# A four-layer decoder trunk in f32 on one core: other opening pieces, chunk 3 loaded into idle tiles, the bias table written from SyncE's queue, lambda later, no low parts on POOL

## The chip, the cores and the metric

The kernel runs on one core of one Trainium2 chip. The metric is the device time of a run in microseconds, from the first to the last instruction of the program on that core; lower is better. Engines are named as the profile names them: PE is TensorE, DVE is VectorE, ACT is ScalarE, POOL is GpSimd, SP is SyncE, which here only issues DMAs. A "queue" is the row of DMAs that one engine issues, in order.

## The reference, cut to what matters

Input x is 256 tokens by 1024. Four residual layers follow each other, the first being the even mixer; only that layer's beginning is touched by what follows.

```
h = x
for layer in range(4):                       # DEPTH 2 in the code: mixer + FFN, twice
    h = h + (even_mixer or odd_mixer)(rmsnorm(h, norm1), w_in, ..., w_out)
    h = h + conv_ffn(rmsnorm(h, ffn_norm), w_in, conv_w, conv_b, w_out)
return rmsnorm(h, final_norm)

even_mixer(h):                               # q,k,v of 8 heads (width 64) and of 4 differential heads
    qa, ka, va, qd, kd, vd = split_cols(h @ w_in, ...)
    o_a = softmax(qa ka' * scale + bias[head] , causal) va
    lam = exp(sum(lp0*lp1)) - exp(sum(lp2*lp3)) + lam_init
    o_b = rmsnorm((softmax(q0 k0') - lam * softmax(q1 k1')) vd) * (1 - lam_init)
    return concat(o_a, o_b) @ w_out
```

The bias of a head is a row of a small table, looked up by the distance of query and key.

## The kernel before, in words

**Weights in chunks.** `PLAN` lists all weights as chunks of 128 x 2048 f32 (1 MB) in the order in which PE wants them: chunk 0 is `eq0` (queries of the first heads), 1 `ek0`, 2 `eq1`, 3 `ek1`, 4 and 5 `eva0`, `eva1` (values), 6 on `eq2` and so forth. `load_raw` brings a chunk from HBM into one of three `raw` buffers by SP's queue. `split_piece` then makes two tiles of each piece: ACT rounds it to `whi` (line 147), and DVE subtracts that from the raw piece to get `wlo` (line 148). For 7 pieces (the second of chunks 6, 9, 12, 15, 51, 57 and 60) the subtraction is POOL's. Activations are split alike, into `xh` and `xl` (tile `xs`). Each product is three passes on PE: whi·xh, whi·xl, wlo·xh. All matmuls of the weights go through the helper at line 123, so they are told apart by the tile that they write: `pd` (queries, keys, FFN), `pv` (values), `pS` (scores), `pT` (transposed probabilities), `acc` (output projection).

**The opening.** PE starts with warm-up matmuls (`warm`). x (tile `hT`) and chunks 0 and 1 come in parts along the contraction, as `FIRST_KS` cuts them: parts of 1, 1, 2, 2, 2 of the eight blocks of 128 rows, so pieces of 128, 128, 256, 256, 256 KB. Of each part `passmajor` runs first whi·xh on both halves of chunk 0 and then on both of chunk 1, then whi·xl in the same order, then wlo·xh. One block gives 4 x 3 = 12 matmuls of 128x256, so a part of two blocks 24. What follows on PE is fixed by hand: `psbt` (bias rows), eq1 (48 matmuls), `pss` (column sums for the norm), the first half of ek1, `psb` (spreads the norm over partitions, from the DVE tile `diag`), the second half of ek1, `pS` of heads 0 to 3, the values of eva0 and eva1 (24 matmuls of 128x512), `pS` of heads 4 to 7, 24 more, then `pT`, eq2 and so on.

**DMA order.** Every DMA from SP or ACT signals on one of eight semaphores in turn; one that takes a semaphore still in use waits for the DMA of eight before to land. In the listings these waits are DMAHW0 to DMAHW7. An engine that waits for a semaphore holds everything behind it in its own order, DMA issues among them.

**The bias table and lambda.** DVE adds the mask to the rows (`ar_t`), ACT's queue writes them to DRAM (`btab`), and ACT's queue reads them back shifted by partition into `Tt` (`bias_load`, heads 0 to 7 in one DMA of 1 MB). DVE's `sc` adds `Tt` to the scores; `ex` are the probabilities, `rd` the inverse of their sum. `lambdas` computes lam on DVE and ACT from `lam_t`, 128 KB on SP's queue; it stands right behind `u3`'s other work.

Of the kernel before, what the change touches and what calls it, by code (L numbers as in the profile page):

```python
# [21 lines left out]
F32 = mybir.dt.float32  # L22
F32R = mybir.dt.float32r
AF = mybir.ActivationFunctionType
ALU = mybir.AluOpType
# [11 lines left out]
NBIAS = 20  # L37
NTAB = 384
# [5 lines left out]
RAW_AHEAD = 3  # L44
LAG = 2
LAGF = 4
WARM = 10
FIRST = 4
FIRST_KS = ((0, 1), (1, 2), (2, 4), (4, 6), (6, 8))
POOLSHARE = 3  # L50
NARROW = 5
TAIL = ((0, 0, 512), (0, 512, 1024), (1, 0, 512), (1, 512, 768), (1, 768, 1024))

# [3 lines left out]
NSMALL = 36  # L57
NCONV = 4 * NF
# [40 lines left out]
PLAN = _plan()  # L99
# [3 lines left out]
def trunk(ctx, tc, x, rel_bias, small, lam_p, wpack, fin_g, onehot, addrow, tab, out):  # L103
    nc = tc.nc
    consts = ctx.enter_context(tc.tile_pool(name="consts", bufs=1))
# [13 lines left out]
    def t2(name, dt=F32, shape=(128, 2, S)):  # L119
        return two.tile(list(shape), dt, name=name, tag="t2")  # L120
# [8 lines left out]
    chunks, raws, splits = {}, {}, {}  # L129
    index = {p[0]: i for i, p in enumerate(PLAN)}  # L130

    def pieces(i):
        n = PLAN[i][4] * PLAN[i][6]
        if i < 2:
            return n, [slice(a * S, b * S) for a, b in FIRST_KS]
        return n, [slice(c, c + 1024) for c in range(0, n, 1024)]

    def load_raw(i, part=None, eng=None):
        n, ps = pieces(i)
        if i not in raws:  # L140
            raws[i] = wraw.tile([128, 2048], F32, name="raw")
        s = slice(0, n) if part is None else ps[part]
        (eng or nc.sync).dma_start(raws[i][:, s], wpack[i, :, s])

    def split_piece(i, s, eng=None):
        hi, lo, raw = splits[i], splits[i, 1], raws[i]
        nc.scalar.activation(hi[:, s], raw[:, s], AF.Copy)  # L147
        (eng or nc.vector).tensor_tensor(lo[:, s], raw[:, s], hi[:, s].bitcast(F32), op=ALU.subtract)  # L148

    def open_split(i):  # L150
        name, nk, ncol = PLAN[i][0], PLAN[i][4], PLAN[i][6]
# [5 lines left out]

    def split_chunk(i):
        open_split(i)
        for n, s in enumerate(pieces(i)[1]):  # L160
            pool = PLAN[i][0][0] in "eo" and n == 1 and i % POOLSHARE == 0 and i > 4
            split_piece(i, s, nc.gpsimd if pool else None)

    raw_at, split_at = [2], [2]

# [28 lines left out]
    def load_x(part, eng):  # L194
        k = slice(*FIRST_KS[part])
        eng.dma_start(hT[:, k], x[:, k])
    load_x(0, nc.sync)
    load_raw(0, 0)
    load_raw(1, 0, nc.scalar)
    load_x(1, nc.sync)  # L200
    load_raw(0, 1, nc.scalar)
    load_raw(1, 1)
    load_x(2, nc.scalar)
    for part in range(2, len(FIRST_KS)):
        if part > 2:
            load_x(part, nc.sync)
        for i in range(2):
            load_raw(i, part)
        if part == 3:
            rb = consts.tile([32, NBIAS], F32)  # L210
            nc.sync.dma_start(rb, rel_bias)
            oh_t = t2("oh_t", shape=(32, NTAB))
            nc.sync.dma_start(oh_t, onehot)
            ar_t = t2("ar_t", shape=(NBIAS + 1, NTAB))
            nc.sync.dma_start(ar_t, addrow)
    load_raw(2, 0)
    load_raw(2, 1)

    lam = consts.tile([128, 4], F32)
    subg = consts.tile([128, 1], F32)  # L220
# [101 lines left out]
    def bias_load(h0, n, at):  # L322
        nc.scalar.dma_start(Tt[:, at:at + n], bass.AP(tensor=btab.tensor, offset=btab.offset + h0 * NTAB,
                                                      ap=[[1, 128], [NTAB, n], [1, S]]))
        return {h0 + i: Tt[:, at + i] for i in range(n)}
# [202 lines left out]
    def v_units(env, cname, vname):  # L528
        ts = []

        def run(tb):
            need(cname + '0')
            c = [chunks[cname + '0'], need(cname + '1')]
            p = bank("pv")
            vjob(p, tb, c)
            t = t2(vname, shape=(128, 512))
            nc.scalar.activation(t, p, AF.Copy, scale=env['r_col'][:, tb:tb + 1])
            ts.append(t)
            if tb == 1:
                env[vname] = ts  # L540
        return [(None, lambda: run(0)), (None, lambda: run(1))]
# [20 lines left out]
    def proj_units(prefix, order, store):  # L562
        box = {}

        def unit(i):
            kt = order[i]

            def run():
                if i == 0:
                    box['acc'] = [bank("acc") for _ in range(4)]  # L570
                proj_tile(box['acc'], store[kt], need(f"{prefix}{kt // 2}"), kt % 2, i == 0, i == KD - 1)
            return kt, run
        return [unit(i) for i in range(KD)], box

    def lambdas():
        for i in range(2):
            nc.vector.tensor_tensor(lam_t[:, 0:64] if i == 0 else lam_t[:, 128:192],
                                    lam_t[:, 128 * i:128 * i + 64],
                                    lam_t[:, 128 * i + 64:128 * i + 128], op=ALU.mult)
            nc.vector.reduce_sum(lam[:, 1 + i:2 + i], lam_t[:, 128 * i:128 * i + 64],  # L580
                                 axis=mybir.AxisListType.X)
        nc.scalar.activation(lam[:, 1:3], lam[:, 1:3], AF.Exp)
        nc.vector.tensor_sub(lam[:, 3:4], lam[:, 1:2], lam[:, 2:3])
        nc.vector.tensor_scalar(lam[:, 0:1], lam[:, 3:4], LAM_INIT, None, op0=ALU.add)

    def even_layer():
        env, store = {}, {}
        T = T0
        box = {}

        def u1():
            c = chunks['eq1']
            p = box['q1'] = bank("pd")
            colmajor([(p[:, 0:S], True, c, 0)])
            split_chunk(3)
            split_at[0] = 4

        def u2():
            p = box['q1']
            colmajor([(p[:, S:], True, chunks['eq1'], 128)])  # L600
            stats1(env)

        def u3():
            box['k1'] = bank("pd")
            colmajor([(box['k1'][:, 0:S], True, chunks['ek1'], 0)])
            p = box['q1']
            stats2(env)
            stats_q(env)
            evac_pair(env, first[0], ('q0', 'q1'), env['r_q'])
            evac_pair(env, first[1], ('k0', 'k1'), env['r_bc'])  # L610
            evac_pair(env, p, ('q2', 'q3'), env['r_q'])
            split_chunk(4)
            split_at[0] = 5
            begin.close()
            lambdas()
            nc.gpsimd.tensor_tensor(sel, iot, iot, op=ALU.mult)
            nc.gpsimd.tensor_scalar(sel, sel, 4096.0, None, op0=ALU.is_equal)
            nc.gpsimd.tensor_tensor(sel, sel, ident, op=ALU.add)
            T.update(bias_load(8, 4, 8))

        def u4():
            colmajor([(box['k1'][:, S:], True, need('ek1'), 128)])
            evac_pair(env, box['k1'], ('k2', 'k3'), env['r_bc'])

        units = [(None, u1), (None, u2), (None, u3), (None, u4)]
        units += v_units(env, 'eva', 'va')
        units += qk_units(env, 'eq2', ('q4', 'q5'), 'r_q') + qk_units(env, 'ek2', ('k4', 'k5'), 'r_bc')
        units += qk_units(env, 'eq3', ('q6', 'q7'), 'r_q') + qk_units(env, 'ek3', ('k6', 'k7'), 'r_bc')
        units += v_units(env, 'evd', 'vd')
        pu, pbox = proj_units('e_o', list(range(8)), store)  # L630
        units += pu
        tasks = [pair_task(env, f"q{i}", f"k{i}", T, 2 * i, 'va', i * 128, store, i)
                 for i in range(4)]
        tasks += [diff_task(env, f"q{4 + i}", f"k{4 + i}", T, 8 + i, 'vd', i * 128, store, 4 + i)
                  for i in range(4)]
        interleave(env, units, tasks, store, FIRST)
        close_phase(pbox['acc'], NORM2[0])
# [336 lines left out]
            split_piece(i, pieces(i)[1][part])  # L974
        passmajor(items, range(a, b))
    pb = bias_rows()
    open_split(2)
    split_piece(2, pieces(2)[1][0])
    bias_add(pb)
    split_piece(2, pieces(2)[1][1])  # L980
    nc.scalar.dma_start(btab, ar_t)
    for j in range(4):
        square_tile(j, hT[:, 2 * j:2 * j + 2], nc.vector)
    for i in (3, 4, 5):
        load_raw(i)
    raw_at[0] = 6
    split_at[0] = 3
    lam_t = t2("lam_t", shape=(128, 256))
    nc.sync.dma_start(lam_t, bass.AP(tensor=lam_p.tensor, offset=lam_p.offset,
                                       ap=[[0, 128], [1, 256]]))  # L990
    ccol = [consts.tile([128, NCONV], F32, name=f"ccol{l}") for l in range(2)]
    for l in range(2):
        nc.sync.dma_start(ccol[l], small[:, NSMALL + l * NCONV:NSMALL + (l + 1) * NCONV])
    tab_t = consts.tile([128, S], F32)
    nc.sync.dma_start(tab_t, tab)
    T0 = bias_load(0, 8, 0)
    even_layer()
    ffn(0, False)
    odd_layer()
# [71 lines left out]
```

## Time and profile before

| | us |
|---|---|
| median of 3 runs (599.11 to 600.66) | 599.34 |
| profiled execution, its own time | 603.9 |
| its span, first to last instruction | 602.1 |
| PE busy (98% of the span) | 589.1 |
| DVE, ACT, POOL busy | 438.7, 349.4, 88.6 |

The profiled execution is one run with the profiler on; its span is what the rows below are cut from, and its time holds 1.8 us around the span. Busy times overlap each other, so they don't add up to the span.

### The profile page before, as it was taken

How to read it: one execution, taken by the hardware profiler on the slowest of the kernel's cores; microseconds unless marked ns; L12 is line 12 of the kernel's file. 1: busy time of each engine (PE TensorE's matmuls, PEld its weight loads, DVE VectorE, ACT ScalarE, POOL GpSimd, SP SyncE). 2: the span in 40 equal slices, each digit the busy share in tenths (PEclk: the TensorE clock that was granted, in tenths of full speed). 3: DMA queues.
4: the chain of work that ended last, by engine and by line, in shares of the span. 5: the costliest groups of instructions: out<-in, count | busy, mean ns of one | idle time of the engine just before them, and what ended most of it. 6: DMA issues, size and time to landing. Idle time of an engine off the chain costs nothing.

```text
span 602.1 us, 10377 instructions
## 1 busy us (share of the span) xinstructions
PE 589.1 (98%) x4078; PEld 542.3 (90%) x4078; DVE 438.7 (73%) x784; ACT 349.4 (58%) x645; POOL 88.6 (15%) x88
## 2 busy tenths in 40 slices
PE   8989999999999999999999999999999999999996
PEld 8878999999999999999999998999988888888885
DVE  5598657689877787777787884658967787777752
ACT  6549557466655565555664574736655566655632
POOL 1010122032111010011142111004111111011110
PEclk9999999999999999999999999999999999999999
DMA  7976644435455545544545333344545545554301
GB/s 235 330 256 222 238 177 157 142 127 189 175 211 210 183 174 203 201 161 169 180 167 205 145 140 140 141 140 158 219 149 209 210 162 188 211 181 170 139 1 71
DMA packets 20250, 106.67 MB, mean 177 GB/s; under 512 B 2463, under 2 KB 6249, under 8 KB 8425
## 3 DMA queue, kind: packets, MB, share of 16 engines
q1 hardware_dynamic: 16396, 101.63, 46.8%
q10 hardware_dynamic: 3644, 3.85, 2.0%
q8 instruction: 32, 0.52, 0.4%
q0 software_dynamic: 160, 0.52, 0.3%
q14 instruction: 18, 0.14, 0.1%
HBM read 104.92 MB, written 1.08 MB: 176 GB/s over the span
## 4 chain that ended last, share of the span: by engine, by line
PE 88%; DVE 5%; DMA 3%; issue 2%; ACT 1%; POOL 1%; POOLq 0%; SPq 0%; ACTq 0%; DVEq 0%
PE pd L123 51%; PE acc L123 26%; PE pv L123 4%; DVE wlo L148 2%; PE pO L123 2%; PE pS L123 2%; DMA lam_t<-in_lam_dram 1%; DMA hT<-in_x_dram 1%; PE puq L123 1%; DVE ex L358 1%; PE pukv L123 0%; DVE sc L348 0%; PE psb L123 0%; PE pT L362 0%; PE pss L123 0%
## 5 line engine op out<-in xcount | busy, mean ns | idle before, releaser
L123 PE MATMUL pd<-xs,whi 128*128 128x256 f32 (+1 forms) x1312 | 329.2, 330 | 1.6 <-ACT whi L147 1.4
L123 PE MATMUL pd<-xs,wlo 128*128 128x256 f32 x928 | 256.6, 281 | 0.0
L148 DVE TENSOR_TENSOR wlo<-raw,whi 128x1024 fp32r<-128x1024 f32 (+2 forms) x190 | 232.2, 1248 | 24.0 <-ACT whi L147 23.9
L123 PEld LDWEIGHTS pd<-xs,whi 128*128 128x128 f32 x1312 | 219.8, 190 | 24.6 <-ACT whi L147 2.6
L147 ACT ACTIVATE whi<-raw 128x1024 fp32r<-128x1024 f32 (+2 forms) x197 | 196.4, 1023 | 58.1 <-PE pd L123 18.2
L123 PEld LDWEIGHTS pd<-xs,wlo 128*128 128x128 f32 x928 | 174.3, 190 | 0.1
L123 PE MATMUL acc<-o,whi 128*128 128x256 f32 x608 | 108.7, 281 | 0.0
L123 PEld LDWEIGHTS acc<-o,whi 128*128 128x128 f32 x608 | 92.7, 188 | 1.0 <-issue 0.2
L123 PE MATMUL acc<-o,wlo 128*128 128x256 f32 x304 | 84.7, 279 | 0.0
L786 POOL TENSOR_TENSOR ge<-ge,gbuf 128x256 f32<-128x256 f32 x44 | 37.1, 844 | 291.2 <-ACT ge L785 291.2
L890 ACT ACTIVATE lowp<-pd 128x256 f32<-128x256 f32 x68 | 25.9, 381 | 79.8 <-PE pd L123 79.8
L891 DVE TENSOR_TENSOR ug<-pd,lowp 128x256 f32<-128x256 f32 x68 | 28.5, 419 | 50.4 <-ACT lowp L890 50.4
L123 PE MATMUL acc<-whi,o 128*128 128x512 f32 (+1 forms) x220 | 58.2, 350 | 0.2 <-ACT o L791 0.2
L123 PEld LDWEIGHTS acc<-o,wlo 128*128 128x128 f32 x304 | 57.1, 188 | 0.0
L123 PEld LDWEIGHTS acc<-whi,o 128*128 128x128 f32 x220 | 38.3, 188 | 7.5 <-ACT o L791 0.7
L123 PE MATMUL acc<-wlo,o 128*128 128x512 f32 (+1 forms) x110 | 38.6, 351 | 0.0
L792 DVE TENSOR_TENSOR o<-ge,o 128x256 fp32r<-128x256 f32 x44 | 19.0, 438 | 21.5 <-ACT o L791 21.5
L773 ACT ACTIVATE t<-gbuf,ccol 128x256 f32<-128x256 f32 x44 | 26.4, 601 | 12.0 <-DVE gbuf L914 10.1
L351 ACT ACTIVATE ex<-sc,nm 128x256 f32<-128x256 f32 (+1 forms) x56 | 24.8, 445 | 14.3 <-DVE nm L348 14.3
L148 POOL TENSOR_TENSOR wlo<-raw,whi 128x1024 fp32r<-128x1024 f32 x7 | 19.0, 2710 | 95.8 <-ACT whi L147 78.7
L791 ACT ACTIVATE o<-ge 128x256 fp32r<-128x256 f32 x44 | 18.4, 418 | 22.8 <-POOL ge L786 22.8
L123 PE MATMUL pv<-whi,xs 128*128 128x512 f32 x96 | 30.2, 395 | 0.0
(152 smaller groups left out, 521.3 us busy)
## 6 DMA issues: line engine op xcount, KB each, us to landing
raw<-in_wpack_dram SPq DMA_DIRECT2D x92, 1024.0 KB, 4.8
Tt<-btab ACTq DMA_DIRECT2D x2, 1024.0 KB, 11.1
raw<-in_wpack_dram SPq DMA_DIRECT2D x6, 256.0 KB, 5.2
raw<-in_wpack_dram SPq DMA_DIRECT2D x3, 512.0 KB, 6.2
hT<-in_x_dram SPq DMA_DIRECT2D x2, 256.0 KB, 4.6
Tt<-btab ACTq DMA_DIRECT2D x1, 512.0 KB
fin<-in_fin_g_dram POOLq DMA_DIRECT2D x2, 256.0 KB, 3.8
out_dram<-y SPq DMA_DIRECT2D x2, 256.0 KB, 2.0
```

The costliest lines, as they stand in the source:

```text
L123: nc.tensor.matmul(o, l, r, start=start, stop=stop, skip_group_check=True)
L147: nc.scalar.activation(hi[:, s], raw[:, s], AF.Copy)
L148: (eng or nc.vector).tensor_tensor(lo[:, s], raw[:, s], hi[:, s].bitcast(F32), op=ALU.subtract)
L351: nc.scalar.activation(e[:, a:b], t[:, a:b], AF.Exp, bias=nm[:, i:i + 1], scale=-1.0, accum_out=den[:, i:i + 1])
L358: nc.vector.tensor_scalar(e[:, a:b], e[:, a:b], rd[:, i:i + 1], None, op0=ALU.mult)
L773: nc.scalar.activation(t1, g[:, 2:], AF.Identity, bias=col(f, 3), scale=col(f, 2))
L786: nc.gpsimd.tensor_tensor(ge, ge, gbuf[f % 3][:, 0, 2:], op=ALU.mult)
L791: nc.scalar.activation(o[:, 0], ge, AF.Copy)
L792: nc.vector.tensor_tensor(o[:, 1], ge, o[:, 0].bitcast(F32), op=ALU.subtract)
L890: nc.scalar.activation(lowp, p[:, S:], AF.Copy)
L891: nc.vector.tensor_tensor(t[:, i], p[:, :S], lowp, op=ALU.add)
```

## The change: what it does

The opening takes four parts of two blocks each (256 KB pieces) instead of five, with another share of them on ACT's queue. Chunk 3 is loaded in four pieces of 256 KB into tiles of the pool `two`, which holds activations later, so it takes no `raw` buffer. `btab` is written from SP's queue, behind the loads of chunks 4 and 5; `Tt` of heads 0 to 7 is read in two DMAs of four heads. The loads of lambda and of two tables are issued ahead of `even_layer`'s unit 6, lambda's arithmetic ahead of unit 10. All low parts are made by DVE. One warm-up matmul fewer.

```diff
-WARM = 10
+WARM = 9
-FIRST_KS = ((0, 1), (1, 2), (2, 4), (4, 6), (6, 8))
-POOLSHARE = 3
+SMALL_RAW = 3
+FIRST_KS = ((0, 2), (2, 4), (4, 6), (6, 8))
...
-    def split_piece(i, s, eng=None):
+    def split_piece(i, s):
         hi, lo, raw = splits[i], splits[i, 1], raws[i]
-        nc.scalar.activation(hi[:, s], raw[:, s], AF.Copy)
-        (eng or nc.vector).tensor_tensor(lo[:, s], raw[:, s], hi[:, s].bitcast(F32), op=ALU.subtract)
+        if isinstance(raw, list):
+            raw = raw[s.start // 512]
+        else:
+            raw = raw[:, s]
+        nc.scalar.activation(hi[:, s], raw, AF.Copy)
+        nc.vector.tensor_tensor(lo[:, s], raw, hi[:, s].bitcast(F32), op=ALU.subtract)
...
     load_x(0, nc.sync)
-    load_raw(0, 0)
-    load_raw(1, 0, nc.scalar)
-    load_x(1, nc.sync)
-    load_raw(0, 1, nc.scalar)
-    load_raw(1, 1)
-    load_x(2, nc.scalar)
+    load_raw(0, 0, nc.scalar)
+    load_raw(1, 0)
+    load_x(1, nc.scalar)
+    load_raw(0, 1)
+    load_raw(1, 1, nc.scalar)
     for part in range(2, len(FIRST_KS)):
-        if part > 2:
-            load_x(part, nc.sync)
+        load_x(part, nc.sync)
         for i in range(2):
             load_raw(i, part)
...
     load_raw(2, 1)
+    raws[SMALL_RAW] = []
+    for part in pieces(SMALL_RAW)[1]:
+        raws[SMALL_RAW].append(t2("raw_t", shape=(128, 512)))
+        nc.sync.dma_start(raws[SMALL_RAW][-1], wpack[SMALL_RAW, :, part])
...
             split_chunk(3)
             split_at[0] = 4
+            T.update(bias_load(0, 4, 0))
+            T.update(bias_load(4, 4, 4))
...
             begin.close()
-            lambdas()
...
+        def loads():
+            T.update(bias_load(8, 4, 8))
+            box['lam'] = late_loads()
+        before(6, loads)
+        before(10, lambda: lambdas(box['lam']))
...
-    nc.scalar.dma_start(btab, ar_t)
+    for i in (4, 5):
+        load_raw(i)
+    nc.sync.dma_start(btab, ar_t)
+    load_raw(6)
     for j in range(4):
         square_tile(j, hT[:, 2 * j:2 * j + 2], nc.vector)
-    for i in (3, 4, 5):
-        load_raw(i)
-    raw_at[0] = 6
+    raw_at[0] = 7
```

SP's own order at the very start, before. `raw_98` is the buffer of chunk 0, `raw_100` that of chunk 1.

```order
1 L196 DMA hT_96<-in_x_dram 128x256
2 L143 DMA raw_98<-in_wpack_dram 128x256
3 L196 DMA hT_96<-in_x_dram 128x256
4 L143 DMA raw_100<-in_wpack_dram 128x256
5 L143 DMA raw_98<-in_wpack_dram 128x512
6 L143 DMA raw_100<-in_wpack_dram 128x512 [waits DMAHW0_49]
7 L196 DMA hT_96<-in_x_dram 128x512 [waits DMAHW2_49]
```

The same place on SP in the changed kernel; by the diff, the first piece of chunk 0 is on ACT's queue, so row 2 is its second piece, and row 4 the first piece of chunk 1.

```order
1 L200 DMA hT_96<-in_x_dram 128x512
2 L144 DMA raw_98<-in_wpack_dram 128x512
3 L200 DMA hT_96<-in_x_dram 128x512
4 L144 DMA raw_100<-in_wpack_dram 128x512
5 L144 DMA raw_98<-in_wpack_dram 128x512
6 L144 DMA raw_100<-in_wpack_dram 128x512 [waits DMAHW1_49]
7 L200 DMA hT_96<-in_x_dram 128x512 [waits DMAHW2_49]
```

The first piece of chunk 1, which stood first on ACT's queue behind a small table, is now fourth on SP's, behind 768 KB; the third part of x and the second piece of chunk 0 have come ahead of it, against the order of the code.

DVE from eq1's split to the first scores, before (`rs` and `diag` belong to the norm, `qk` are the scaled queries and keys).

```order
22 L148 TENSOR_TENSOR wlo<-raw,whi 128x1024 x2
23 L247 TENSOR_SCALAR rs<-pss 128x2
24 L577 TENSOR_TENSOR lam_t<-lam_t 128x64 x2
25 L263 TENSOR_TENSOR diag<-ident,r_col 128x256
26 L580 TENSOR_REDUCE lam<-lam_t 128x1 x2
27 L281 COPY r_bc<-psb 128x256
28 L583 TENSOR_TENSOR lam<-lam 128x1
29 L559 TENSOR_SCALAR r_q<-r_bc 128x256
30 L584 TENSOR_SCALAR lam<-lam 128x1
```

The same place on DVE in the changed kernel.

```order
19 L153 TENSOR_TENSOR wlo<-raw_t,whi 128x512 x4
20 L252 TENSOR_SCALAR rs<-pss 128x2
21 L268 TENSOR_TENSOR diag<-ident,r_col 128x256
22 L286 COPY r_bc<-psb 128x256
23 L564 TENSOR_SCALAR r_q<-r_bc 128x256
24 L518 TENSOR_TENSOR qk<-pd,r_q 128x512
```

The six instructions of lambda are gone from between `rs` and `qk`; nothing stands between `rs` and `diag` now.

SP from the last load of chunk 3 on, in the changed kernel.

```order
17 L222 DMA raw_t<-in_wpack_dram 128x512 [waits DMAHW5_49]
18 L144 DMA raw<-in_wpack_dram 128x2048 [waits DMAHW6_49,DVE_49]
19 L144 DMA raw<-in_wpack_dram 128x2048 [waits DMAHW7_49,DVE_49]
20 L996 DMA btab<-ar_t 21x384 [waits DMAHW0_49,DVE_49]
21 L144 DMA raw<-in_wpack_dram 128x2048 [waits DMAHW1_49,Activation_49]
```

`btab`, which stood on ACT's queue ahead of the squares (`sqt`), now stands on SP's behind 2 MB of chunks 4 and 5.

## Rows read from the trace of the kernel before

**Rows 1.** The page's busy time, share of the span and instructions of each engine.

```profile
PE 589.1 (98%) x4078; PEld 542.3 (90%) x4078; DVE 438.7 (73%) x784; ACT 349.4 (58%) x645; POOL 88.6 (15%) x88
```

**Rows 2.** Windows: start:end, length, busy us (instructions) by engine, PE clock, DMA, GB/s.

```profile
5.30:10.41 5.11, 3.55 (x27) 3.15 (x26) 2.78 (x8) 2.80 (x8) 0.00 (x0) 1.00 0.88 299
10.41:20.00 9.59, 9.59 (x74) 8.84 (x74) 6.76 (x11) 6.49 (x11) 0.00 (x0) 1.00 0.92 301
20.00:31.40 11.40, 9.50 (x77) 9.17 (x76) 7.25 (x13) 6.11 (x8) 0.73 (x1) 1.00 0.91 325
...
60.00:300.00 240.00, 240.00 (x1739) 224.87 (x1738) 179.18 (x299) 142.16 (x258) 35.97 (x34) 1.00 0.50 181
300.00:590.00 290.00, 289.19 (x1936) 263.70 (x1935) 212.34 (x363) 165.05 (x297) 45.33 (x42) 1.00 0.45 160
```

**Rows 3.** Waits of PE: tile, releaser, us in total, times, longest.

```profile
PE psb L123 <- DVE diag L263: 1.9, 1, 1.9
PE pd L123 <- ACT whi L147: 1.4, 1, 1.4
PE pT L362 <- DVE rd L353: 1.2, 1, 1.2
```

**Rows 4.** Timeline of PE, opening: start, us, what, [idle before it, releaser].

```profile
1.04 4.63 PE L123 MATMUL warm<-ones 128*128 128x128 f32 x20 [1.04 <-DVE gbuf L761]
...
10.41 0.91 PE L123 MATMUL pd<-xs,whi 128*128 128x256 f32 x5 [1.41 <-ACT whi L147]
```

**Rows 5.** Timeline of SP, opening: when DMAs were issued.

```profile
2.09 1.65 SPq L143 DMA_DIRECT2D raw<-in_wpack_dram  x3
```

**Rows 6.** DMA issues, 0 to 3 us: queue, count, KB each, us to landing.

```profile
raw<-in_wpack_dram SPq DMA_DIRECT2D x1, 256.0 KB, 6.1
```

**Rows 7.** Tile raw, 0 to 9 us: time of its DMAs to landing.

```profile
DMA to landing us min/median/max: 3.6/5.0/6.1
```

**Rows 8.** Chain of waits in the opening: start, us, what.

```profile
9.84 0.53 ACT whi L147
```

**Rows 9.** Timeline of PE around eq1, 18.8 to 22.6 us.

```profile
19.27 0.82 PE L123 MATMUL psbt<-oh_t,rb 32*20 32x384 f32 x2
...
21.85 0.39 PE L123 MATMUL pd<-xs,wlo 128*128 128x256 f32 x1
22.08 0.41 PE L123 MATMUL pd<-xs,whi 128*128 128x256 f32 x2
```

**Rows 10.** Timeline of DVE, 18 to 43 us.

```profile
25.14 2.35 DVE L148 TENSOR_TENSOR wlo<-raw,whi 128x1024 fp32r<-128x1024 f32 x2
27.41 0.15 DVE L247 TENSOR_SCALAR rs<-pss 128x2 f32<-128x2 f32 x1
30.66 0.36 DVE L577 TENSOR_TENSOR lam_t<-lam_t 128x64 f32<-128x64 f32 x2 [3.11 <-DMA lam_t<-in_lam_dram]
30.94 0.42 DVE L263 TENSOR_TENSOR diag<-ident,r_col 128x256 f32<-128x256 f32 x1
...
34.74 6.83 DVE L148 TENSOR_TENSOR wlo<-raw,whi 128x1024 fp32r<-128x1024 f32 x4
```

**Rows 11.** Timeline of POOL, 33 to 43 us.

```profile
37.48 3.00 POOL L148 TENSOR_TENSOR wlo<-raw,whi 128x1024 fp32r<-128x1024 f32 x1 [9.11 <-ACT whi L147]
```

**Rows 12.** Timeline of PE, 34.5 to 58 us, where groups start.

```profile
36.41 0.73 PE L123 MATMUL pv<-whi,xs 128*128 128x512 f32 x2
...
42.75 1.58 PE L123 MATMUL pS<-qk 64*128 64x256 f32 x16
44.26 0.73 PE L123 MATMUL pv<-whi,xs 128*128 128x512 f32 x2
...
49.86 0.27 PE L362 MATMUL pT<-ident,ex 128*128 128x128 f32 x1
```

**Rows 13.** DMA issues, 20 to 31 us.

```profile
Tt<-btab ACTq DMA_DIRECT2D x1, 1024.0 KB, 12.9
...
lam_t<-in_lam_dram SPq DMA_DIRECT2D x1, 128.0 KB, 8.4
```

**Rows 14.** Windows at the end, columns as in Rows 2.

```profile
596.20:599.00 2.80, 0.00 (x0) 0.00 (x0) 1.03 (x3) 1.20 (x3) 0.55 (x1) 1.00 0.00 0
...
599.60:600.50 0.90, 0.00 (x0) 0.00 (x0) 0.00 (x0) 0.00 (x0) 0.00 (x0) 0.50 1.02 389
```

More of the change, by code (lines that the diff above doesn't have):

```diff
@@ L135, in pieces @@
             return n, [slice(a * S, b * S) for a, b in FIRST_KS]
-        return n, [slice(c, c + 1024) for c in range(0, n, 1024)]
+        step = 512 if i == SMALL_RAW else 1024
+        return n, [slice(c, c + step) for c in range(0, n, step)]
     def load_raw(i, part=None, eng=None):
@@ L159, in split_chunk @@
         open_split(i)
-        for n, s in enumerate(pieces(i)[1]):
-            pool = PLAN[i][0][0] in "eo" and n == 1 and i % POOLSHARE == 0 and i > 4
-            split_piece(i, s, nc.gpsimd if pool else None)
+        for s in pieces(i)[1]:
+            split_piece(i, s)
     raw_at, split_at = [2], [2]
@@ L197, in trunk @@
     load_x(0, nc.sync)
-    load_raw(0, 0)
-    load_raw(1, 0, nc.scalar)
-    load_x(1, nc.sync)
-    load_raw(0, 1, nc.scalar)
-    load_raw(1, 1)
-    load_x(2, nc.scalar)
+    load_raw(0, 0, nc.scalar)
[3 more added lines that the diff above has]
+    load_raw(1, 1, nc.scalar)
     for part in range(2, len(FIRST_KS)):
-        if part > 2:
-            load_x(part, nc.sync)
+        load_x(part, nc.sync)
         for i in range(2):
             load_raw(i, part)
[L209 to L215, printed above, removed]
-    load_raw(2, 0)
+    load_raw(2, 0)
+    rb = consts.tile([32, NBIAS], F32)
+    nc.sync.dma_start(rb, rel_bias)
+    oh_t = t2("oh_t", shape=(32, NTAB))
+    nc.sync.dma_start(oh_t, onehot)
+    ar_t = t2("ar_t", shape=(NBIAS + 1, NTAB))
+    nc.sync.dma_start(ar_t, addrow)
     load_raw(2, 1)
+    raws[SMALL_RAW] = []
+    for part in pieces(SMALL_RAW)[1]:
+        raws[SMALL_RAW].append(t2("raw_t", shape=(128, 512)))
+        nc.sync.dma_start(raws[SMALL_RAW][-1], wpack[SMALL_RAW, :, part])
     lam = consts.tile([128, 4], F32)
@@ L573, in proj_units, with lambdas @@
         return [unit(i) for i in range(KD)], box
-    def lambdas():
+    def lambdas(lam_t):
         for i in range(2):
@@ L587, in even_layer @@
         env, store = {}, {}
-        T = T0
+        T = {}
         box = {}
@@ L618, in u3 @@
             nc.gpsimd.tensor_tensor(sel, sel, ident, op=ALU.add)
-            T.update(bias_load(8, 4, 8))
         def u4():
@@ L629, in even_layer, with before @@
         units += v_units(env, 'evd', 'vd')
+        def before(n, do):
+            wants, fn = units[n]
+            units[n] = wants, lambda: (do(), fn())
+        def loads():
[3 more added lines that the diff above has]
+        before(10, lambda: lambdas(box['lam']))
         pu, pbox = proj_units('e_o', list(range(8)), store)
@@ L976, in trunk, with late_loads @@
     pb = bias_rows()
-    open_split(2)
-    split_piece(2, pieces(2)[1][0])
+    split_chunk(2)
     bias_add(pb)
-    split_piece(2, pieces(2)[1][1])
-    nc.scalar.dma_start(btab, ar_t)
+    for i in (4, 5):
+        load_raw(i)
+    nc.sync.dma_start(btab, ar_t)
+    load_raw(6)
     for j in range(4):
         square_tile(j, hT[:, 2 * j:2 * j + 2], nc.vector)
-    for i in (3, 4, 5):
-        load_raw(i)
-    raw_at[0] = 6
+    raw_at[0] = 7
     split_at[0] = 3
-    lam_t = t2("lam_t", shape=(128, 256))
-    nc.sync.dma_start(lam_t, bass.AP(tensor=lam_p.tensor, offset=lam_p.offset,
-                                       ap=[[0, 128], [1, 256]]))
     ccol = [consts.tile([128, NCONV], F32, name=f"ccol{l}") for l in range(2)]
-    for l in range(2):
-        nc.sync.dma_start(ccol[l], small[:, NSMALL + l * NCONV:NSMALL + (l + 1) * NCONV])
     tab_t = consts.tile([128, S], F32)
-    nc.sync.dma_start(tab_t, tab)
-    T0 = bias_load(0, 8, 0)
+    def late_loads():
+        lam_t = t2("lam_t", shape=(128, 256))
+        nc.sync.dma_start(lam_t, bass.AP(tensor=lam_p.tensor, offset=lam_p.offset,
+                                         ap=[[0, 128], [1, 256]]))
+        for l in range(2):
+            nc.sync.dma_start(ccol[l], small[:, NSMALL + l * NCONV:NSMALL + (l + 1) * NCONV])
+        nc.sync.dma_start(tab_t, tab)
+        return lam_t
     even_layer()
```

## The prediction

> **What bounds the kernel now.** First the page's head: PE is busy 589.1 us, 98% of the span, and no other engine passes 73% [rows 1]. So an edit pays only where PE stands still, and the table by windows says where [rows 2]: from 60 to 300 us nowhere, from 300 to 590 us for 0.8 us in all, but for 1.6 of 5.11 us up to 10.41 and for 1.9 of 11.40 us up to 31.40. The change touches just the beginning; what it does later has cover. Third, PE's waits name the causes [rows 3]: `psb` waits 1.9 us for `diag`, `pd` 1.4 us for a `whi` piece, `pT` 1.2 us for DVE. All three lie in the first 60 us. Since PE has no slack afterwards, a microsecond won or lost before reaches the end of the kernel whole.
>
> The 1.4 us of `pd` ends at 10.41 us [rows 4]; from there to 20 us PE has no gap, 74 matmuls in 9.59 us [rows 2]. So the opening is decided once the data are there by about 10 us: from then on matmuls of 128x256 follow each other every 0.12 us (72 from 10.41 to 19.27, when `psbt` begins [rows 9]).
>
> **The change part by part**, each as a shift of PE against before.
>
> **1. The opening's loads: +1.6 us (bounds -0.6 to +2.5).** The first group of matmuls needs the first piece of chunk 0 and, after 4 matmuls, that of chunk 1. In the changed order this piece is fourth on SP's queue, behind 768 KB, while ACT's queue moves 768 KB of its own. When does it land? The nearest row is the one 256 KB piece that was issued in the first 3 us: second of the three issues that begin at 2.09 us and take 1.65 us together, so issued near 2.6, and 6.1 us to landing [rows 5, 6], near 8.7. By the listing it was fifth on SP's queue with 512 KB ahead. At the 299 GB/s that all queues moved from 5.30 to 10.41 us [rows 2] the 256 KB more are 0.9 us; the issue is one place earlier, about 0.4 us. I take 8.7 + 0.9 - 0.4 = 9.2 us. `whi` of 512 columns follows, 0.53 us [rows 8], so the fifth matmul starts near 9.8. Then 20 matmuls of the first part (2.4 us) and three parts of 24 (8.6 us) end near 20.8 to 20.9, against 19.27: +1.6. In general the end is the landing + 11.6 us, so a landing at 7.6 us costs nothing. Bounds: the weight pieces issued in the first 9 us took 5.0 us at the median [rows 7], and from an issue near 2.1 us that is 7.0 (-0.6); if SP's queue gets less than that share, one more slot of 0.9 us, 10.1 (+2.5). I stay by the 6.1 us row, since it has the most bytes ahead of it. The warm-up matmul less falls into a stretch in which PE waits for data anyway.
>
> **2. Lambda out of the way: -1.9 us (bounds 0 to -1.95).** `rs` was done at 27.56 us, yet DVE stood idle 3.11 us until 30.66: in its order the two `lam_t` products come before `diag`, and `lam_t` landed 8.4 us after its issue [rows 10, 13]. `diag` came 0.28 us later, then `psb`. With lambda gone from there (the order shows `rs` and `diag` as neighbours) the chain is `rs`, POOL's power (0.73 us is all that POOL did in this window [rows 2]) and `diag` 0.42 us: ready by 28.8, while PE reached `psb` 1.9 us before 31.4, at 29.5. So the wait goes whole, with 0.7 us to spare, and what is late next is nothing on this path; the lower bound holds if the chain slips by the 1.9 us. Lambda itself goes behind unit 10; its loads are issued at unit 6, and DVE does the same 1 us of work where PE has matmuls queued.
>
> **3. A small stop in eq1: -0.1 us (0 to -0.2).** The matmul at 21.85 us is 0.23 us ahead of the next, where 0.12 is the rule [rows 9]: `wlo`'s second half was late since the bias add stood between the halves. Now both halves come first.
>
> **4. Low parts off POOL, before the scores: -0.7 us (0 to -0.75).** Four `wlo` of eva0 and eva1 took DVE 6.83 us; two of the same shape took 2.35, so four are 4.7 [rows 10]. POOL ran its own `wlo` from 37.48 to 40.48, inside them [rows 11]. PE felt it: the first 24 `pv` took 6.34 us (36.41 to 42.75), the next 24 took 5.60 (44.26 to 49.86) [rows 12]. That difference of 0.74 us can go.
>
> **5. The transposes: -0.5 us (0 to -1.2).** Ahead of the last `pT`, DVE sheds 2.1 us by edit 4 and gets one more `wlo`, 1.2 us, since the second piece of chunk 6 was POOL's. DVE is ahead by 0.9 us and PE by 0.7, so of the 1.2 us that `pT` waits [rows 3] little goes by that alone; but two `wlo` now stand behind the first `ex` of their group, which helps the earlier `pT`. I take 0.5.
>
> **6. What should cost nothing.** Seven POOL pieces become DVE work, 7 x 1.2 = 8 us, five of them behind 60 us, where DVE is busy 179 of 240 and 212 of 290 us [rows 2] and chunks are split ahead; without that cover each would cost its 1.2 us. `btab` behind chunks 4 and 5 means 2 MB ahead of it, 6.5 us at 325 GB/s [rows 2]: issued near 21 us, it lands near 27 to 28. ACT holds for it before the reads of `Tt`; behind those are the `whi` of eva0 and eva1, 4 us of work for `pv` at about 36. `Tt`, 12.9 us for 1 MB [rows 13], is then there by 34 for the first four heads and by 41 for the others, while DVE comes to them near 40 and 44. The slack of 3 us is the cover. Chunk 3 in four pieces moves the same bytes.
>
> **Sum:** 1.6 - 1.9 - 0.1 - 0.7 - 0.5 = -1.6 to -1.7 us. The rows are from the profiled execution, whose own time is 603.9 us where the three runs have 599.34 at the median, 0.8% less. A shift of 1.7 us does not change by that ratio, so 603.9 becomes 602.2, and the median 599.34 - 1.7 = 597.6 us.
>
> **The rivals.**
>
> **A, the piece lands early.** If the queues share so that chunk 1's piece lands at 7 to 8 us, term 1 is -0.6 to +0.4 and the total -2.8 to -3.8: 595.5 to 596.5 us. For it: the median of 5.0 us [rows 7]. Against it: the 768 KB ahead.
>
> **B, PE's clock is low when the opening resumes.** After 4 matmuls PE would stand still from about 6.6 to 9.8 us. At the end of the kernel, with the last matmul done before 596.2 us, the granted clock still reads 1.00 up to 599 us and 0.50 from 599.6 us on, the lower level of 1.2 GHz [rows 14]. What low means for PE the warm-up shows: 20 matmuls of 128 columns in 4.3 us, 0.21 us each [rows 4], though later ones of twice the width need 0.12. If the clock falls in the new gap and stays low as long as the warm-up took, 4.3 us hold 18 matmuls at 0.24 us that would take 2.15: 2.1 us lost, the total +0.4, 599.8 us. Against it: the gap of 1.41 us [rows 4] lowered nothing, and at the end 2.8 us without a matmul passed at 1.00. The Trainium skill, in "TensorE: Matmul & The Clock Gate", section "HAM oscillation — how this bites in real kernels", tells of groups of matmuls that are shorter than the wait for their data: the clock is throttled in the wait, and the next group starts slow. By that rule the time is B's; the trace agrees that standing still lowers the clock [rows 14], and shows no gap of 3 us in the middle of work.
>
> **C, the saved waits come back.** DVE is what PE waits for up to 57 us, and it gets work. If `pT` waits longer by what `psb` and `pv` wait less, terms 1 and 3 remain with half of 2: 599.5 to 600.5 us. Against it: the 3.11 us in which DVE only stood [rows 10].
>
> **D, slower: the bias table is late.** ACT is held until `btab` lands. Its 4 us of `whi` are due at 36 us, so each microsecond of landing behind 32 delays `pv` by one. To give back the 1.7 us and lose 1.8 more, it must land behind 35.5 us, 14 us after its issue; the longest row here is 12.9 us, for 1 MB [rows 13]. Then 601.2 us or more.
>
> **How the numbers follow.** Forecast (landing between 8.5 and 9.8 us): 0.42, its own range 596.9 to 598.2. A 0.20, B 0.18, C 0.12, D 0.08. A measurement of this kernel tells about 0.3%, 1.8 us, from no change, so the border of "faster" is 597.5, in the middle of the forecast. Sixty in a hundred of the forecast with A make faster 0.45; the rest of the forecast, B and most of C are the same, 0.43; D and the worst of B and C are slower, 0.12. The range, 595.0 to 600.6, leaves out D and the far ends of A.
>
> **What would show it.** Step 1 is right if the fifth `pd` matmul starts near 9.8 us and `psbt` near 20.9, wrong if `psbt` starts before 19.5 or after 22. B is right if the matmuls behind the gap stand 0.24 us apart. Step 2 is right if `psb` doesn't wait, step 4 if the four `wlo` take 4.7 us and the two groups of `pv` are equally long, step 5 if `pT` waits 0.7 us or less in all. The whole fails if a new wait of PE above 1 us appears between 20 and 60 us, or any behind 60.

## The result, and the profile after

The changed kernel takes 603.55 us at the median of four runs (603.03 to 603.62), the kernel before 599.95 us beside it: a ratio of 1.0059, 95% interval 1.0041 to 1.0076. It is slower by 3.6 us, outside the range that was given and to the other side. Yet the two traces alone seem to say "no change": the profiled execution after has a span of 601.7 us where that of before had 602.1. Both halves of this need explaining, the 3.6 us and why the trace of before hid them.

The table by windows after, columns as in [rows 2]; the first two rows are cut where the matmuls' distance changes.

```profile
9.00:14.00 5.00, 4.99 (x23) 4.99 (x24) 5.00 (x10) 4.91 (x11) 0.00 (x0) 1.00 1.04 373
14.00:22.40 8.40, 8.40 (x71) 8.31 (x69) 4.11 (x6) 6.86 (x12) 0.00 (x0) 1.00 0.99 379
...
60.00:300.00 240.00, 240.00 (x1739) 225.00 (x1740) 181.06 (x302) 142.63 (x259) 27.63 (x31) 1.00 0.50 181
300.00:590.00 290.00, 289.18 (x1934) 263.60 (x1933) 213.59 (x366) 164.52 (x296) 37.82 (x38) 1.00 0.45 160
```

Behind 60 us nothing moved (PE idle 0.8 us, as before). But from 9 to 14 us PE is "busy" 4.99 of 5.00 us with 23 matmuls, 0.21 us each, and from there to 22.4 us with 71 in 8.40 us, 0.12 each: the same matmuls at half the pace. A busy share cannot show this; the counts beside it do. The column of the granted clock reads 1.00 in both windows, but this trace's records of the clock begin at 14.08 us, so before that it cannot be trusted. Only the starts of the matmuls tell. The timeline of PE after, opening:

```profile
1.04 4.21 PE L123 MATMUL warm<-ones 128*128 128x128 f32 x18 [1.04 <-DVE gbuf L776]
6.98 1.22 PE L123 MATMUL pd<-xs,whi 128*128 128x256 f32 x4 [1.73 <-ACT whi L152]
9.01 2.93 PE L123 MATMUL pd<-xs,whi 128*128 128x256 f32 x12 [0.81 <-ACT whi L152]
...
22.44 0.82 PE L123 MATMUL psbt<-oh_t,rb 32*20 32x384 f32 x2
```

The first piece of chunk 1 landed at 8.30 us (chain of waits: issued 2.10, 6.20 us), and matmul 5 starts at 9.01, earlier than forecast. But 12 matmuls take from 9.01 to 11.73. `psbt` comes at 22.44 instead of 19.27 us [rows 9], 3.2 us late where +1.6 was forecast. The waits of PE after:

```profile
PE pd L123 <- ACT whi L152: 2.5, 2, 1.7
PE pT L367 <- DVE lam_t L582: 1.1, 1, 1.1
```

The wait of `psb` [rows 3] is gone, as forecast, and so is one of 0.4 us that `pv` had before: `psb` starts at 32.35 us without a wait, and the first `pv` group takes 5.67 us (37.24 to 42.91) instead of 6.34 [rows 12]. A wait of 1.1 us at `pT` stayed.

### The profile page after: what moved, and what is told of

It reads as the page before. It is cut to its first block, busy times and chain, and to the rows that moved or that the text cites. A ratio compares the mean times of both kernels' runs of the same rounds, so it can differ in the third digit from the quotient of the medians.

```text
span 601.7 us, 10374 instructions
## 1 busy us (share of the span) xinstructions
PE 590.3 (98%) x4076; PEld 544.2 (90%) x4076; DVE 441.5 (73%) x791; ACT 348.7 (58%) x645; POOL 69.6 (12%) x81
## 4 chain that ended last, share of the span: by engine, by line
PE 88%; DVE 4%; issue 3%; POOL 2%; ACT 2%; DMA 1%; SPq 0%; POOLq 0%; ACTq 0%; DVEq 0%
PE pd L123 51%; PE acc L123 26%; PE pv L123 4%; PE pO L123 2%; PE pS L123 2%; DVE wlo L153 2%; DMA raw<-in_wpack_dram 1%; PE puq L123 1%; POOL sqt L245 1%; DVE ex L363 1%; PE pukv L123 0%; DVE sc L353 0%; PE pT L367 0%; PE psb L123 0%; PE pss L123 0%
## 5 line engine op out<-in xcount | busy, mean ns | idle before, releaser
L153 DVE TENSOR_TENSOR wlo<-raw,whi 128x1024 fp32r<-128x1024 f32 (+1 forms) x193 | 233.8, 1238 | 23.6 <-ACT whi L152 23.5
L152 ACT ACTIVATE whi<-raw 128x1024 fp32r<-128x1024 f32 (+1 forms) x193 | 193.7, 1031 | 60.8 <-PE pd L123 20.9
L800 ACT ACTIVATE ge<-t 128x256 f32<-128x256 f32 x44 | 17.9, 410 | 15.3 <-DVE t L795 15.3
```

What stands on the lines that cost most here:

```text
L152: nc.scalar.activation(hi[:, s], raw, AF.Copy)
L153: nc.vector.tensor_tensor(lo[:, s], raw, hi[:, s].bitcast(F32), op=ALU.subtract)
L800: nc.scalar.activation(ge, t3, AF.Gelu)
```

## The experiments

All in one table: the median time, the median of the runs of the kernel before that stand beside it, and from each one's profile the start of `psbt`, the span, and the span less `psbt`, which is everything behind the opening. Each median is over ten to twelve runs, but for three of the first row, four of the second and of e9, six of e11 and five of e13.

| kernel | us | before | psbt | span | span less psbt |
|---|---|---|---|---|---|
| before, first profile | 599.34 | | 19.27 | 602.1 | 582.8 |
| changed, first profile | 603.55 | 599.95 | 22.44 | 601.7 | 579.3 |
| e1 before again | 600.15 | 600.31 | 18.68 | 598.0 | 579.3 |
| e2 changed, 18 warm-up | 601.06 | 600.31 | 19.98 | 599.2 | 579.2 |
| e3 changed, old opening | 600.59 | 600.31 | 20.95 | 600.6 | 579.7 |
| e4 before, lambda late | 600.04 | 600.31 | 18.93 | 598.5 | 579.6 |
| e5 changed, POOL's pieces back | 603.29 | 600.82 | 20.90 | 600.3 | 579.4 |
| e6 changed, piece earlier | 602.25 | 600.82 | 20.58 | 599.8 | 579.2 |
| e7 same, 13 warm-up | 600.96 | 600.82 | 19.42 | 598.7 | 579.3 |
| e8 same, POOL's pieces back | 601.13 | 600.82 | 19.75 | 599.1 | 579.4 |
| e9 before, new opening | 609.99 | 600.17 | 22.48 | 609.2 | 586.7 |
| e10 before, no POOL pieces | 600.77 | 600.17 | 19.24 | 598.9 | 579.7 |
| e11 before, bridge | 606.81 | 600.17 | 19.09 | 604.7 | 585.6 |
| e12 changed, old opening, bridge | 600.67 | 600.17 | 19.33 | 598.9 | 579.6 |
| e13 lambda late, new opening | 601.82 | 600.35 | 21.23 | 599.9 | 578.7 |
| e14 same, 18 warm-up | 600.76 | 600.35 | 19.77 | 598.7 | 578.9 |
| e15 lambda late, 13 warm-up | 600.33 | 600.35 | 19.08 | 598.5 | 579.4 |
| e16 changed again | 603.11 | 600.34 | 22.06 | 601.3 | 579.2 |
| e17 changed, 10 warm-up | 602.69 | 600.34 | 21.52 | 600.8 | 579.3 |

The last column is the key: but for three profiles everything behind `psbt` takes 578.7 to 579.7 us, whichever parts of the change are in. A span is that of one execution and can lie off its row's median: those of e3 and e9 are the longest of their runs, those of e5, e7, e11 and e13 the shortest.

**e1: the kernel before, again.** 

> The kernel before once more, unchanged, with a profile of its own. Theory P (the profiled execution of before, 603.9 us, was some 4 us longer than its usual runs, and part of the waits read there are not in the usual runs): span near 598 us, the wait of psb under 0.5 us instead of 1.9, or the opening over before 19.3 us. Rival Q (every execution has these waits, the 4 us lie elsewhere): psb waits 1.9 us again, pT 1.2 us again, psbt begins at 19.3 us, whatever the span.

DVE's timeline around the norm, to be held against [rows 10], and PE's where `psb` starts:

```profile
27.81 0.15 DVE L247 TENSOR_SCALAR rs<-pss 128x2 f32<-128x2 f32 x1
28.63 0.36 DVE L577 TENSOR_TENSOR lam_t<-lam_t 128x64 f32<-128x64 f32 x2 [0.67 <-DMA lam_t<-in_lam_dram]
28.91 0.42 DVE L263 TENSOR_TENSOR diag<-ident,r_col 128x256 f32<-128x256 f32 x1
```

```profile
29.55 0.59 PE L123 MATMUL psb<-diag,ones 128*128 128x256 f32 x2
```

Here lambda is late by 0.67 us and not 3.11, since it landed 7.0 us after its issue and not 8.4, in an opening 0.6 us earlier. `psb` does not wait at all, the `pv` group takes 5.67 us, `pT` waits 0.2 us. Theory P holds: the waits that the prediction meant to remove were those of one of the longer executions, 603.9 us against a median of 599.3. Such executions are not rare: beside the experiments the kernel before took more than 602.5 us in 21 of 128 runs.

**e2: 18 warm-up matmuls.** `WARM = 9` becomes `WARM = 18`. 

> The changed kernel with 18 warm-up matmuls instead of 9, so that PE is busy until the first piece is split at about 7 us. Theory C (the clock: PE stands still after the warm-up, the first 28 matmuls of the opening run 0.21 us apart until 14 us): they run 0.12 us apart, psbt begins at 20.2 instead of 22.4 us, time 603.55 - 2.2 = 601.3 us. Rival D (the data set the pace): psbt at 22.4 us, 603.5 us.

Its timeline of PE:

```profile
1.04 6.80 PE L123 MATMUL warm<-ones 128*128 128x128 f32 x36 [1.04 <-DVE gbuf L776]
7.60 0.72 PE L123 MATMUL pd<-xs,whi 128*128 128x256 f32 x4
8.77 1.69 PE L123 MATMUL pd<-xs,whi 128*128 128x256 f32 x12 [0.45 <-ACT whi L152]
```

The same 12 matmuls take 1.53 us (8.77 to 10.30) instead of 2.72, `psbt` is 2.46 us earlier, the time 2.5 us less. The data came no sooner. Theory C holds.

**e3 and e4: the old opening in the changed kernel; lambda late in the kernel before.**

```diff
-FIRST_KS = ((0, 2), (2, 4), (4, 6), (6, 8))
+FIRST_KS = ((0, 1), (1, 2), (2, 4), (4, 6), (6, 8))
...
-    load_raw(0, 0, nc.scalar)
-    load_raw(1, 0)
+    load_raw(0, 0)
+    load_raw(1, 0, nc.scalar)
```

> The changed kernel with the opening of before (five parts, its load order, 10 warm-up matmuls); chunk 3, btab, lambda and the low parts stay as changed. Theory C: the opening alone costs 3.2 us, so 603.55 - 3.2 = 600.4 us and psbt at 19.3 us, no different from before if theory P holds. If instead the 3.5 us that the rest seemed to win in the two traces are real in usual runs: 599.95 - 3.5 = 596.5 us.

> The kernel before with one part of the change: lambda's and the tables' loads at unit 6, lambda's arithmetic at unit 10. If the wait of psb (1.9 us) is in usual runs of before: 598.0 us. Theory P: the wait is mostly absent in usual runs, 599.5 to 600 us, no change.

Ratios to before: 1.0005 (0.9990 to 1.0020) and 0.9997 (0.9984 to 1.0010). So neither the rest of the change nor lambda's new place moves the time by more than these intervals, about 1 us. Lambda late may still avoid the worst executions: its ten runs end at 600.95 us, those of before beside it at 604.79, and with e15 none of 21 such runs passes 602.5 us. That lambda is what the long executions wait for is not shown; of these only the first profile was seen. The profile of e3 shows the clock at work, in windows and in PE's timeline:

```profile
12.00:15.40 3.40, 3.40 (x18) 3.40 (x18) 3.02 (x7) 2.83 (x6) 0.00 (x0) 0.51 0.83 225
15.40:20.00 4.60, 4.60 (x40) 4.60 (x39) 2.37 (x4) 2.57 (x4) 0.00 (x0) 0.99 1.01 363
```

```profile
10.60 2.71 PE L123 MATMUL pd<-xs,whi 128*128 128x256 f32 x16 [1.91 <-ACT whi L152]
```

PE stood still 1.91 us, resumed at full pace, and 1.5 us later fell to half for 3.4 us, granted clock 0.51. It was the longest of this kernel's runs (602.4 us).

**e5: POOL's seven pieces given back.** `split_piece(i, s)` becomes `split_piece(i, s, nc.gpsimd if pool else None)`, as before. 

> The changed kernel with the seven low parts given back to POOL. Theory L (the last pT wait of 1.1 us is chunk 6's second low part, now on DVE ahead of the last probabilities): the wait falls to about 0.2 us, time 603.55 - 0.9 = 602.6 us. Rival M (the wait is lambda's arithmetic, which the wait's name shows): 1.1 us stays, 603.5 us.

The wait at `pT` fell to 0.6 us in all, not to 0.2, 0.5 us came up at `pS`, and the part behind `psbt` stayed at 579.4 us. Theory L is right in part on the wait and wrong on the gain.

**e6, e7 and e8: chunk 1's first piece earlier, more warm-up, POOL's pieces back.**

```diff
-    load_raw(1, 0)
-    load_x(1, nc.scalar)
+    load_raw(1, 0, nc.scalar)
+    load_x(1, nc.sync)
```

> The changed kernel, only the first piece of chunk 1 put behind that of chunk 0 on ACT's queue, ahead of the rest, and x's second part on SP's. Theory C (the clock): the stop inside the first group is gone, but the first matmuls, from about 6.5 us on, still run 0.21 us apart for some 4 us, psbt near 20.5 us, about 601.5 us. Rival D (the late piece is the whole cost): psbt near 18.5 us, 599.7 us.

> The same with 13 warm-up matmuls, so that PE is busy until the first piece is there. Theory C: the first group runs 0.12 us apart, psbt near 18.3 us, about 599.3 us. Rival D: as in the run without the extra warm-up, since the data set the pace.

> The same with the seven low parts on POOL again, the version that should beat both kernels. Theories C and L together: 0.9 us under the run with 13 warm-up matmuls, about 598.4 us, against 600.0 to 600.3 us of the kernel before. If L is wrong, the same time as that run.

With the earlier piece PE resumes at 8.37 instead of 9.01 us, though still at half pace, up to 10.7 us; it takes 602.25 us where e5 beside it takes 603.29. The longer warm-up gives 1.3 us more (600.96), POOL's pieces nothing (601.13). None beats the kernel before, and theory C's 599.3 and 598.4 us were missed: the first group does run 0.12 us apart, but a stop of 0.77 and 1.37 us stayed inside it. Theory L failed with e8. Why POOL's pieces don't pay, DVE's and POOL's timelines of e8 show:

```profile
32.88 5.72 DVE L154 TENSOR_TENSOR wlo<-raw,whi 128x1024 fp32r<-128x1024 f32 x4
```

```profile
31.73 2.39 POOL L154 TENSOR_TENSOR wlo<-raw,whi 128x1024 fp32r<-128x1024 f32 x1 [3.87 <-ACT whi L153]
```

In e1 POOL's piece lay beside the scores, and DVE's four took less:

```profile
32.77 4.62 DVE L148 TENSOR_TENSOR wlo<-raw,whi 128x1024 fp32r<-128x1024 f32 x4
```

```profile
37.08 2.59 POOL L148 TENSOR_TENSOR wlo<-raw,whi 128x1024 fp32r<-128x1024 f32 x1 [8.30 <-ACT whi L147]
```

The overlap of 1.2 us costs DVE 1.1 us, about what the piece would take on DVE itself.

**e9 and e11: the new opening, and a bridge, in the kernel before.** e9 puts the new opening there; e11 has `WARM = 12` and six warm-up matmuls more behind the second part.

> The kernel before with the opening of the change alone (four parts, its load order, 9 warm-up matmuls). Theory C (the opening, by the low clock and the late first part, is the whole loss): 600.2 + 3.3 = 603.5 us, psbt near 22 us with its first matmuls 0.21 us apart. Rival R (the rest of the change loses too): clearly less, 602 us or under.

> The kernel before with 12 warm-up matmuls and six more of the same behind the second part, into PE's idle time before the third, so that PE never stands still for over half a microsecond. If low clock in some runs is what makes the kernel before range from 598.8 to 604.8 us: a median near 599.3 us and a narrower range. If not: 600.2 to 600.8 us and the same range.

Both missed, and for a reason that neither theory had. DVE's timeline of e9:

```profile
28.00 0.42 DVE L239 TENSOR_TENSOR sqt<-sqt 128x256 f32<-128x256 f32 x1
31.95 0.36 DVE L574 TENSOR_TENSOR lam_t<-lam_t 128x64 f32<-128x64 f32 x2 [3.53 <-DMA lam_t<-in_lam_dram]
32.23 0.21 DVE L577 TENSOR_REDUCE lam<-lam_t 128x1 f32<-128x64 f32 x1
32.35 2.35 DVE L148 TENSOR_TENSOR wlo<-raw,whi 128x1024 fp32r<-128x1024 f32 x2
```

The scheduler orders what is not fixed by hand, and here lambda's products came ahead of ek1's low parts, where before they stood behind them. PE waited 3.5 us for `wlo` in e9 and 2.8 us in e11. And behind these waits, in the middle of work, the clock fell to half in both. PE's timeline and a window of e9, then a window of e11:

```profile
33.63 0.58 PE L123 MATMUL pd<-xs,wlo 128*128 128x256 f32 x1 [3.54 <-DVE wlo L148]
```

```profile
33.60:38.40 4.80, 4.77 (x22) 4.78 (x23) 1.95 (x6) 2.21 (x3) 0.73 (x1) 0.50 0.66 233
```

```profile
31.50:34.80 3.30, 3.30 (x16) 3.11 (x15) 0.67 (x4) 2.00 (x2) 0.42 (x1) 0.50 0.80 283
```

From `psbt` to `psb` e9 takes 5.1 us more than e1: 3.0 of longer waiting and 2.1 of half pace. The opening of e9 itself is that of the change, `psbt` at 22.48 us.

**e10: all low parts on DVE, in the kernel before.** 

> The kernel before with all low parts on DVE. Theory N (a low part on DVE costs it as much as the POOL one did by standing beside DVE's): 600.2 us, no change; the last pT wait goes from 0.2 to about 1.1 us, and what is won elsewhere makes up for it. Rival L (the extra low part ahead of the last probabilities costs what its wait says): 601.1 us. Step 4 of the prediction: 599.5 us.

Ratio 1.0011 (0.9997 to 1.0026): not told apart from no change, and L's 0.9 us not excluded. Its profile has the wait of 1.1 us at `pT`, named `ex`. In the changed kernel the same wait is named `lam_t`, but the timeline of DVE there shows what came first:

```profile
54.79 1.21 DVE L153 TENSOR_TENSOR wlo<-raw,whi 128x1024 fp32r<-128x1024 f32 x1
55.91 0.55 DVE L363 TENSOR_SCALAR ex<-ex,rd 128x256 f32<-128x256 f32 x2
56.37 0.36 DVE L582 TENSOR_TENSOR lam_t<-lam_t 128x64 f32<-128x64 f32 x2
```

PE resumes at 56.60 us, 0.15 us after the second `ex` ends, as it does in e1 and e10, where no lambda stands there. The extra `wlo` ahead of `ex` is the delay; lambda only stands next in line.

**e12: the bridge with the old opening in the changed kernel.** 

> The changed kernel with the opening of before, and the same 12 and six matmuls. By theory C its opening is that of the run above, so the difference to it is what the rest of the change is worth: 0 by the distance of psbt to pO (37.5 us in both kernels). If the rest wins its 0.5 to 0.8 us (no wait for the low part of ek1) after all: 598.7 us, under the kernel before.

600.67 us, all twelve runs between 600.3 and 601.1, the narrowest of all rows with ten runs or more, but no faster than the kernel before: 1.0009 (0.9995 to 1.0023). The six matmuls keep the clock up, but the third part starts at 10.47 us here, 0.65 us later than in e1. Against e11 it tells nothing, since that run lost for another reason.

**e13 to e15: without lambda in the way.** e13 is e4 with the new opening and 9 warm-up matmuls, e14 the same with 18, e15 e4 with 13.

> The kernel before with lambda late and the opening of the change (four parts, its load order, 9 warm-up matmuls), so that lambda can't stand ahead of ek1's low part on DVE. Theory C (the opening is the whole loss of the change): as the changed kernel, 603.5 us, psbt near 22.4 us, span less psbt 579.3 us. Rival R (the rest of the change loses as well): clearly below 603 us.

> The same with 18 warm-up matmuls. Theory C: 2.4 us less than the run with 9, about 601.0 us, psbt near 20 us. If the low clock was a matter of the other parts of the change: no difference.

> The kernel before with lambda late and 13 warm-up matmuls: the opening of before with a longer warm-up, without the six matmuls in its gap. If the clock that rises late in some runs of before costs it something: 599.5 us and no run above 601, the version that beats both. If the gaps of this opening let the clock fall in spite of it: 600.0 us with the same range as without the three more matmuls.

The new opening alone takes 601.82 us where the median beside it is 600.35; the ratio on record, which is not the quotient of these two medians, is 1.0040 (1.0026 to 1.0055). By medians that is a smaller loss than the change's, as rival R said; by the ratio, from five runs, it lies between the 1.0059 of the first series and the 1.0032 of e16. So a loss in the rest of the change is not shown. With 18 warm-up matmuls it takes 600.76. In e15 13 warm-up matmuls gain nothing: 600.33 us, with runs up to 602.36. In e13 the clock was low for 3.5 us, shorter than in the changed kernel, which is most of the difference in `psbt`. Window of e13:

```profile
8.90:12.40 3.50, 3.50 (x19) 3.50 (x19) 3.49 (x8) 3.36 (x8) 0.00 (x0) 0.51 1.06 400
```

**e16 and e17: the change again, and with 10 warm-up matmuls.**

> The changed kernel once more, unchanged. If its 603.0 to 603.6 us hold on another chip: 603.5 us and psbt near 22.4 us. If the length of the low clock differs from job to job, as the same opening in the kernel before suggests (601.8 us): between 601.8 and 603.6 us, and psbt follows the time, span less psbt staying at 579.3 us.

> The changed kernel with 10 warm-up matmuls instead of 9, the one that the change took away. Theory C in its narrow form (the last warm-up matmul decides whether the clock rises before the first real ones): as with 18, 601 us. In its wide form (the two stops behind the warm-up let it fall again): no better than the changed kernel beside it, within 0.5 us.

e16 takes 602.0 to 603.7 us, 1.0032 (1.0012 to 1.0053): the loss stands in a second series, a little smaller. Its first matmuls run 0.21 us apart up to 13.1 us, those of the first profile up to 14.1, of e13 up to 12.4, and `psbt` follows: 22.06, 22.44, 21.23. With the tenth warm-up matmul the median is 0.4 us lower (602.69), within the spread of both. In its profile the four matmuls between the stops ran at full pace and those behind the second stop at half, so the stops decide, not that one.

## Why the prediction was wrong, point by point

**The opening (step 1).** The data part was mis-sized the safe way: the piece landed at 8.30, not 9.2 us, and at full clock `psbt` would be near 20.0 us, as e2 shows, +0.7 by [rows 9] and not +1.6. What failed is that term 1 put the clock at nothing, on the ground of "Against it" in rival B: that a gap of 1.41 us lowered nothing, and that 2.8 us at the end passed at 1.00. The new opening makes two stops with four matmuls between them. In both profiles of the changed kernel, and in e6, those four were slow already, and no matmul before 14.1, 13.1 and 10.7 us ran at full pace: there the clock had not risen yet; a fall in the gap, which is B's way, is not what these profiles show. In e5, e9, e13 and e17 the four ran at full pace, and the group behind the second stop was slow, at once or after three matmuls. PE's timeline of e5:

```profile
6.16 0.74 PE L124 MATMUL pd<-xs,whi 128*128 128x256 f32 x4 [1.21 <-ACT whi L153]
8.38 2.93 PE L124 MATMUL pd<-xs,whi 128*128 128x256 f32 x12 [1.48 <-ACT whi L153]
```

In the first profile 23 matmuls took 5.07 us (9.01 to 14.08), where the same 23 took 2.85 in e2: 2.2 us lost. Rival B's price, 2.1 us, came out, though by luck in its terms (18 matmuls, 0.24 us apart, for the 4.3 us of the warm-up); the loss belonged in the sum. The Trainium skill ("TensorE: Matmul & The Clock Gate", "HAM oscillation — how this bites in real kernels"), which was cited for B, tells that a group shorter than the wait for its data is followed by a slow one. e5, e9 and e13 agree: four matmuls in 0.74 us, then waits of 1.48, 1.73 and 1.68 us. e8 does not: after a wait of 1.37 us it went on at full pace. In e17 a second wait of 0.60 us was enough, behind a first of 2.19.

**Lambda, the low parts, the transposes (steps 2, 4, 5).** Between the two traces they came as forecast: `psb` -1.9, `pv` -0.7, `pT` -0.4 us (54.18 to 56.88 against 54.20 to 57.26), and the small stop of eq1 -0.16. The failing step is the last of the sum, "A shift of 1.7 us does not change by that ratio": the profiled execution was 4.6 us over the median, and 3.5 of these lay behind `psbt` (582.8 against 579.3 us in e1), in the very waits that were to be removed. Against e1 the gains are 0.16 us in eq1 and 0.8 us up to `psb` (2.95 us from ek1's start, against 3.75 with a wait of 0.5 for `wlo`), the loss 1.0 us at `pT` (2.70 from 54.18, against 1.72 from 51.38). Sum by the last column of the table: 0.

**What should cost nothing (step 6).** Six of the seven pieces did, as far as PE shows no wait for them. Chunk 6's, the one that the text counted on DVE's side of step 5, is the 1.0 us at `pT`. The bias table was in time: both reads of `Tt` were issued by 25.8 us and landed some 7 us later, so rival D never came near. Rival C was right in its form, since a wait of DVE came back at `pT`.

**In all.** `psbt` came 3.2 us later than in the first profile of before and 3.8 later than in e1: 2.2 us of the low clock, the rest of later data, 1.0 or 1.6. Behind `psbt` gain and loss cancel against e1. That is the 3.6 us of the first series. In e16 `psbt` is 0.4 us earlier, and the loss by medians 0.8 us smaller; the rest of that difference is within the spread. Held against the forecast, term 1 missed by 2.2 us (+3.8 for +1.6, against e1) and terms 2 to 5 by 3.2 (0 for -3.2).

What stays open: why the slow matmuls lasted from 2.3 us (e6) to 5.9 us (e9) in different runs; why the clock was up behind the first stop in e13, whose warm-up had run at half pace throughout, and not in the changed kernel, whose warm-up had the same length; and why the remainders of e13 and e14 (578.7 and 578.9 us) lie under all others. One profile of each doesn't carry an answer.

## What to carry to other kernels

Before a wait is priced, see whether the profiled execution is a usual one: 603.9 us beside a median of 599.3 says that some of its waits may be its own, and a second profile of the same kernel costs less than a wrong change. In this opening, which waits for data, five smaller pieces (e3, 600.59 us) beat four larger ones (603.55 and 603.11), unless a longer warm-up filled the wait (e2, 601.06). So an idle stretch is priced with the clock that it may hold down, not with its own length alone. An instruction that waits for a DMA in an engine's order is a risk even when it is usually in time; e9 and e11 show what one place earlier costs, the wait and then the clock.

## What the runs showed of the hardware that was not expected

With PE at work from 1.04 us on, the moment at which its matmuls go from half to full pace differs from run to run of nearly the same opening: 4.1 us in e1, 5.1 in e12, 5.8 in e15, 6.4 in e2. In the changed kernel's first profile, with its stops, it is 14.1. A fall need not come in the gap: in e3 and in e11 it came 1.5 us after work had resumed, behind waits of 1.91 and 2.80 us, while in e9 the matmuls behind a wait of 3.54 us were slow from the first. And much the same gaps end either way: in e5 PE waited 1.21 us, ran four matmuls, waited 1.48 us and went on at half pace; in e8 it waited 0.66 us, ran four, waited 1.37 us and went on at full pace. A wait of 1.92 us, that of `psb` in the first profile of before, lowered nothing; one of 1.91 us in e3 did.
